# A transformer-and-RWKV layer on one core: one of ten triangular inverses moved from the input projection to the attention stage

## The chip, the cores and the metric

The kernel runs on one core of one Trainium2 chip. The metric is the device time of one execution in microseconds. TensorE (PE) multiplies matrices, VectorE (DVE), ScalarE (ACT) and GpSimd (POOL) work element by element, and SP issues most of the DMAs. Every engine takes its instructions in the order that was fixed when the program was compiled, so an instruction that waits holds up all that stands behind it on its engine, and a DMA that waits on SP holds up all later DMAs of SP.

## The reference

One layer over 2048 latent tokens of width 1024 with a prefix of 256 context tokens. A modulated layer norm feeds one input projection, whose columns go to eight neighbourhood-attention heads (a window of 8 by 16 grid cells plus all context keys) and to eight RWKV-7 heads, which scan the tokens in both directions:

```
S = S * w_t - (S kk_t)(kk_t * a_t)^T + v_t k_t^T ;  y_t = S r_t
```

Both halves are joined, projected, normalised, and followed by a squared-ReLU MLP and a second norm.

## The kernel before, in words

The scan is done in 36 chunks of 64 tokens for each direction d. Within a chunk the delta rule needs the inverse of a triangular 64x64 matrix for each head. These inverses are made ahead of the scan by `solve(d, q0)` (L731 on). The first number is the direction, the second the first of 32 chunk-and-head-pair entries, four to a chunk: `(0, 96)` covers chunks 24 to 31, `(0, 112)` chunks 28 to 35.

A solve is a generator; each call of it emits one piece. In order: DMAs that bring the matrices from the DRAM tensor LB into the tile `mp` (L741) and a clearing of part of the DRAM tensor XB (L749); 31 pairs of DVE instructions, a product into `stmp` (L758) and a row sum into `xp` (L759), which grow from 1 to 961 elements a partition and each read what the one before wrote; an ACT copy `yp` (L763); DMAs out to XS, YS and XB and back in transposed (L767 to L789); a pause of `swait` calls; two rounds of 64 small matmuls, each with an ACT copy behind it (L798, L799); and the DMAs of the last block to XB (L802). All tiles of a solve come from a pool with one buffer each, so two solves overlap little.

The ten solves are spread over the program by the table `SOLVES` (L38). The **input projection** (`phase1`) goes over the tokens in three parts; each is a list of 27 jobs, each of which projects 128 columns of w_in (L448, L466) and works on the result on DVE and ACT: shifts, RWKV terms, rotary embedding (L710 to L715, which ends in a DMA to KR or Q). After each of a job's two pieces `side()` calls the current solve once. Two solves run beside the second part and three beside the third. With `swait` 2 a solve takes 17 calls.

The **attention stage** (first half of `tail`) interleaves three things: 134 steps of `attention()`, of which the first 128 each begin one attention tile (`front`: the product of queries and keys L979, with context keys L982, maximum, exponent, and one scaling on POOL, L997) and finish an earlier one (`back`); 28 steps of the scan in both directions (`chain_pre` loads and prepares a chunk, its inverse `xz` from XB included, L1111 to L1147; `chain_main` advances the state, L1166 to L1195); and `side()`, called after each attention step, which advances the five solves that are left. With `SWAIT` 6 a solve takes 21 calls there. Before step 1 of the attention its own loads must be made and split: keys `kr` (L909 to L911), queries `qz` (L951 to L954), biases `bu` and `bm` (L930 to L934). After the stage the output projection begins (`out_init`), whose tiles take the place in memory of those of the solves and the attention.

The scheduler of the tile framework puts the instructions of all engines into their final order from the order of the program text, from their dependences, and from a timeline of its own.

Of the kernel before, what the change touches and what calls it, by code (L numbers as in the profile page):

```python
# [34 lines left out]
XAT = ("K", 1)  # L35
SPEED = 1

SOLVES = [[(0, 0), (1, 0)], [(1, 112), (1, 96), (0, 96)], [(0, 32), (0, 64), (1, 64), (1, 32), (0, 112)]]  # L38
ASTEPS = 128 + LAG + 4
MID = 28  # L40
SWAIT = 6
# [18 lines left out]
class Kern:  # L60
# [151 lines left out]
    def phase1(self):  # L212
        nc, tc, a = self.nc, self.tc, self.a
        with ExitStack() as es:
# [28 lines left out]
            for n, (sb, b) in enumerate(jobs):  # L243
                if b == jobs[0][1]:
# [3 lines left out]
                    if nxt > 1:  # L248
                        self.sq += [self.solve(*x) for x in SOLVES[nxt - 2]]
                if n == 4:  # L250
# [555 lines left out]
    def tail(self):  # L806
        nc, tc, a = self.nc, self.tc, self.a
        eb, ex = ExitStack(), ExitStack()
        with ExitStack() as ep:
            with ExitStack() as eo:  # L810
                with ExitStack() as ec:

                    self.yacc = [self.pool(ec, "yacc0", 1, side="right").tile([128, 4, 1024], F32, name="yacc0"), None]
                    self.seen = [False] * NCH
                    self.ch1 = self.pool(ec, "ch1", 1, side="right")
                    self.ch2 = self.pool(ec, "ch2", 2, side="right")
                    self.psG = self.pool(ec, "psG", 2, space=PSUM, side="right")
                    self.psR = self.pool(ec, "psR", 1, space=PSUM, side="right")
                    order = [list(range(36)), [3, 2, 1, 0] + list(range(35, 3, -1))]
                    with ExitStack() as ea:  # L820
                        self.sv = self.pool(ea, "sv2", 1)
                        self.at1 = self.pool(ea, "at1", 1)
                        self.at2 = self.pool(ea, "at2", 2)
                        self.psA = self.pool(ea, "psA", 1, space=PSUM)
                        self.psS, self.psname = self.psG, "psg"
                        self.sq = [self.solve(*x) for x in SOLVES[2]]
                        self.speed = 1
                        self.swait = SWAIT
                        self.attn_init()
                        self.chain_init()  # L830
                        at = self.attention()
                        n = 0
                        next(at)
                        self.chain_pre(0, order)
                        next(at)
                        n = 2
                        for s in range(MID):
                            self.chain_pre(s + 1, order)
                            for d in range(2):
                                want = (2 * s + d + 1) * 134 // (2 * MID)  # L840
                                h = (n + want) // 2
                                while n < h:
                                    next(at)
                                    n += 1
                                    self.side()
                                self.chain_main(d, s, order[d])
                                while n < want:
                                    next(at)
                                    n += 1
                                    self.side()  # L850
                        for _ in at:
                            pass
                        assert not self.sq
                    self.psO = self.pool(ep, "psO", 4, space=PSUM)
                    self.chain_pre(MID + 1, order)
                    self.out_init(eo)
                    tiles = self.out_tiles()
                    n = 0
                    for s in range(MID, 36):
                        if MID < s < 35:  # L860
                            self.chain_pre(s + 1, order)
                        for d in range(2):
                            self.chain_main(d, s, order[d])
                            want = 12 * (2 * (s - MID) + d + 1) // (2 * (36 - MID))
                            while n < want:
                                next(tiles)
                                n += 1
                self.psN = self.pool(ep, "psN", 4, space=PSUM, side="right")
                self.base = self.pool(eb, "base", 1, side="right")
                self.xp = self.pool(ex, "xp", 1, side="right")  # L870
                self.uk = self.base.tile([128, 8, 256], F32, tag="uk", name="uk")
                self.xu = {}
                for pr in MORD[:3]:
                    self.xu[pr] = [self.xp.tile([128, 4, 512], F32R, name="x%s%d" % (v, pr)) for v in "hl"]
                self.w1 = {}
                self.w1load(0)
                todo = list(range(8))
                more = True
                while more:
                    for m in todo[:2]:  # L880
                        self.xstep(0, m // 2, m % 2)
                    del todo[:2]
                    more = next(tiles, 0) is None
                assert not todo
        with ExitStack() as e1:
            self.mlp1(e1)
        ex.close()
        with ExitStack() as em:
            self.mlp2(em)
        eb.close()  # L890
# [1036 lines left out]
```

## Time and profile before

| | us |
|---|---|
| median of three runs | 3481.47 |
| the three runs | 3479.99 to 3482.71 |
| the profiled execution, its own time | 3474.77 |
| its span, first to last instruction | 3472.9 |
| PE busy | 3196.9 (92%) |
| DVE busy | 2610.7 (75%) |
| mean granted TensorE clock | 0.96 |

By the trace the input projection ends about 1004 us from the span's start, the attention stage runs to about 1797 us, the output projection follows, and then the two MLP products. The profiled execution is 6.7 us shorter than the median, so every sum below is made against 3474.77 and then carried to the median. "Busy" counts an engine as busy while an instruction is in it. The bound of a stage is read from the waits in that stage, not from the busy shares of the whole span.

### The profile page before, as it was taken

The page shows a single profiled execution, that of the slowest core. Times are in us where ns is not written, and L with a number is a line of the kernel's source. Part 1 is how long each engine was busy: PE and PEld are TensorE (multiplying, and loading weights), DVE is VectorE, ACT ScalarE, POOL GpSimd, SP SyncE. Part 2 cuts the span into 40 slices and gives each one's busy share as a digit, 9 for nine tenths or more (in the row PEclk, how much of TensorE's full clock was granted, in tenths as well). Part 3 has the DMA queues.
Part 4 walks back from the last instruction along what each step waited for, and adds up shares of the span by engine and source line. Part 5 has one row for each costly group of instructions (what it writes and reads, how often), then busy time and mean ns, then how long its engine had stood idle before and what let it go on. Part 6 is the DMA issues. An engine that isn't in the chain of part 4 may idle for free.

```text
span 3472.9 us, 65271 instructions
## 1 busy us (share of the span) xinstructions
PE 3196.9 (92%) x25176; PEld 2602.5 (75%) x25176; DVE 2610.7 (75%) x4907; ACT 1523.3 (44%) x2891; POOL 507.8 (15%) x535
## 2 busy tenths in 40 slices
PE   7999999899957988999979987999999989999998
PEld 3878888789755766776766765777788868888886
DVE  5567977979697668668559867867776757899888
ACT  4555565456433544444442122343433344337433
POOL 0000000000013454544433321000000000010001
PEclk9999999899978999999999988999999999999999
DMA  7487366636776464554354646566644445546442
GB/s 251 133 244 215 90 172 174 195 86 172 188 179 152 110 147 117 134 126 118 97 165 149 182 151 204 196 198 209 217 146 157 141 181 168 162 148 223 143 154 76
DMA packets 765338, 561.67 MB, mean 162 GB/s; under 512 B 380412, under 2 KB 653564, under 8 KB 763620
## 3 DMA queue, kind: packets, MB, share of 16 engines
q1 hardware_dynamic: 691738, 523.14, 51.7%
q10 hardware_dynamic: 73290, 34.37, 3.5%
q8 instruction: 198, 3.24, 0.4%
q14 instruction: 112, 0.92, 0.1%
HBM read 359.70 MB, written 197.66 MB: 160 GB/s over the span
## 4 chain that ended last, share of the span: by engine, by line
PE 66%; DVE 15%; DMA 10%; issue 3%; ACT 3%; SPq 3%; ACTq 0%; POOL 0%; DVEq 0%; POOLq 0%
PE psm L448 13%; PE psa L1524 10%; PE psqb L1722 7%; PE psqa L1722 7%; PE psb L1524 5%; PE ops L1339 3%; PE pse L1524 2%; DMA ks<-AR 2%; PE psv L1044 2%; PE psm L466 2%; PE psg L1134 1%; DVE stmp L758 1%; PE pst L1015 1%; PE psl L979 1%; DMA qz<-Q 1%
## 5 line engine op out<-in xcount | busy, mean ns | idle before, releaser
L448 PE MATMUL psm<-xh,wh 128*128 128x386 f32 (+1 forms) x1104 | 381.0, 347 | 15.5 <-ACT row L451 10.3
L448 PE MATMUL psm<-xl,wh 128*128 128x386 f32 (+1 forms) x1104 | 381.1, 345 | 2.2 <-DVE xl L419 2.1
L448 PE MATMUL psm<-xh,wl 128*128 128x386 f32 (+1 forms) x1104 | 376.9, 341 | 0.0
L448 PEld LDWEIGHTS psm<-xh,wh 128*128 128x128 f32 x1104 | 210.2, 191 | 41.5 <-ACT row L451 18.8
L448 PEld LDWEIGHTS psm<-xl,wh 128*128 128x128 f32 x1104 | 210.6, 191 | 17.6 <-DVE xl L419 7.6
L448 PEld LDWEIGHTS psm<-xh,wl 128*128 128x128 f32 x1104 | 210.5, 191 | 5.0 <-issue 3.7
L1524 PE MATMUL psa<-xh,w1h 128*128 128x512 f32 x512 | 204.6, 400 | 9.2 <-ACT w1h L1455 4.8
L1524 PE MATMUL psa<-xl,w1h 128*128 128x512 f32 x512 | 203.2, 397 | 0.0
L1788 POOL TENSOR_TENSOR acc<-acc,g 128x1024 f32<-128x1024 f32 x8 | 28.9, 3639 | 1188.4 <-DVE acc L1731 1188.4
L1524 PE MATMUL psa<-xh,w1l 128*128 128x512 f32 x512 | 202.2, 396 | 0.0
L1672 ACT CAST ah<-al 128x1024 fp32r<-128x1024 f32 x98 | 102.9, 1050 | 222.8 <-DMA al<-HU 197.0
L1673 DVE TENSOR_TENSOR al<-al,ah 128x1024 fp32r<-128x1024 f32 x98 | 121.4, 1239 | 88.4 <-ACT ah L1672 88.3
L758 DVE TENSOR_TENSOR stmp<-mp,xp 128x9 f32<-128x9 f32 (+30 forms) x310 | 168.0, 542 | 23.8 <-DMA mp<-LB 11.0
L434 DVE TENSOR_TENSOR wl<-wst,wh 128x1024 fp32r<-128x1024 f32 x81 | 98.8, 1219 | 89.1 <-ACT wh L433 76.0
L1455 ACT CAST w1h<-w1s 128x512 fp32r<-128x512 f32 x96 | 59.6, 621 | 239.4 <-DVE w1s L1444 82.2
L1722 PE MATMUL psqa<-uh,ah 128*128 128x512 f32 x400 | 155.0, 391 | 4.2 <-ACT uh L1628 3.2
L1722 PE MATMUL psqb<-uh,ah 128*128 128x512 f32 x384 | 149.8, 393 | 9.8 <-ACT uh L1628 9.8
L1134 PE MATMUL psg<-ks,bkc 64*64 64x128 f32 (+1 forms) x1152 | 99.2, 292 | 63.3 <-DMA ks<-AR 61.0
L1722 PE MATMUL psqa<-ul,ah 128*128 128x512 f32 x400 | 157.3, 393 | 0.0
L1722 PE MATMUL psqa<-uh,al 128*128 128x512 f32 x400 | 156.8, 392 | 0.0
L759 DVE TENSOR_REDUCE xp<-stmp 128x3 f32<-128x9 f32 (+30 forms) x310 | 154.0, 497 | 3.4
L1722 PE MATMUL psqb<-ul,ah 128*128 128x512 f32 x384 | 151.0, 393 | 0.0
(393 smaller groups left out, 8890.5 us busy)
## 6 DMA issues: line engine op xcount, KB each, us to landing
al<-HU SPq DMA_DIRECT2D x106, 512.0 KB
wst<-in_w_in SPq DMA_DIRECT2D x81, 512.0 KB
w<-in_mlp_w SPq DMA_DIRECT2D x32, 1024.0 KB
wp<-in_mlp_w SPq DMA_DIRECT2D x32, 1024.0 KB
wmod<-in_w_mod SPq DMA_DIRECT2D x48, 512.0 KB
HU<-p SPq DMA_DIRECT2D x96, 256.0 KB
HU<-s SPq DMA_DIRECT2D x84, 256.0 KB
bkc<-BK SPq DMA_DIRECT2D x36, 512.0 KB
```

What stands on the lines that cost most here:

```text
L434: nc.vector.tensor_tensor(wl, w, f32(wh), ALU.subtract)
L448: nc.tensor.matmul(ps[:, :y - x], lhsT=s[:, k, :], rhs=m[:, k, x:y], start=(i == 0), stop=(i == 23))
L466: nc.tensor.matmul(ps[:, :y - x], lhsT=s[:, k, :], rhs=m[:, k, lo + x:lo + y], start=(i == 0), stop=(i == 23))
L758: nc.vector.tensor_tensor(tv, mp[:, i:i + 1, lo:lo + n].to_broadcast([128, n, n]), xp[:, lo:lo + n, lo:lo + n], ALU.mult)
L759: nc.vector.tensor_reduce(xp[:, lo:lo + n, i], tv, AX.X, ALU.add)
L1044: nc.tensor.matmul(cell["ps"][hs, i0:i0 + n, :], lhsT=vt[:, hs], rhs=x, start=first, stop=last, skip_group_check=True)
L1134: nc.tensor.matmul(ps[u, p, 0:w], lhsT=bk[o, d, p, u], rhs=ks[h][o, d, p, 0:w], start=True, stop=True)
L1339: nc.tensor.matmul(ps, lhsT=x[:, k, :], rhs=w[:, k, c], start=(i == 0), stop=(i == 23))
L1524: nc.tensor.matmul(ps, lhsT=w[:, k, :], rhs=x[:, k, :], start=(i == 0 and pr in (1, 5, 2)), stop=(i == 11), skip_group_check=True)
L1672: fs += [lambda: nc.scalar.copy(ah, f32(al)), fb[0], lambda: V.tensor_tensor(al, f32(al), f32(ah), ALU.subtract), fb[1]]
L1673: lambda: V.tensor_tensor(al, f32(al), f32(ah), ALU.subtract), fb[1]]
L1722: nc.tensor.matmul(ps, lhsT=x[:, c, s], rhs=y[:, c, :], start=(i == 0 and new), stop=(i == 5 and end), skip_group_check=True)
```

## The change

Solve `(0, 96)` leaves the third part's list and goes to the attention's, before `(0, 112)`. The attention's list, now six, is not called before its sixth step.

```
-SOLVES = [[(0, 0), (1, 0)], [(1, 112), (1, 96), (0, 96)], [(0, 32), (0, 64), (1, 64), (1, 32), (0, 112)]]
+SOLVES = [[(0, 0), (1, 0)], [(1, 112), (1, 96)], [(0, 32), (0, 64), (1, 64), (1, 32), (0, 96), (0, 112)]]
+
+SFIRST = 6
...
                         at = self.attention()
+                        sq, self.sq = self.sq, []
                         n = 0
...
                                 while n < h:
                                     next(at)
                                     n += 1
+                                    if n == SFIRST:
+                                        self.sq = sq
                                     self.side()
                                 self.chain_main(d, s, order[d])
                                 while n < want:
                                     next(at)
                                     n += 1
+                                    if n == SFIRST:
+                                        self.sq = sq
                                     self.side()
```

In the attention stage the solves' calls began at step 3 and ended at step 107 (five times 21 calls). They now begin at step 6, and the last call of the six is at step 131 of 134. Line numbers of the changed kernel are 2 higher up to the attention stage and 7 higher behind it; the rows below print each kernel's own.

The rows below show how the compiled order moves. First the SP queue at the start of the attention stage, from the loads of the first scan chunk on (`ks`, `bkc`, `SV`, `xz` belong to the scan, `vw` to the attention; `XS`, `YS`, `svx`, `svs` and `XB<-yp` to the moved solve). Before:

```order
L1121 DMA SV<-VT 64x4x64 x4
L1123 DMA xz_11143<-XB 128x2x256
L918 DMA vw<-VN 32x8x128 x7
L767 DMA XS_82<-xp 128x1024
L918 DMA vw<-VN 32x8x128 x3
L768 DMA YS_84<-yp 128x1024
L773 DMA XB<-yp 32x32x32 x4
L785 DMA svx<-LB 32x16x32 x4
L788 DMA svs<-XS_82 32x16x32
L789 DMA svs<-YS_84 32x16x32
```

After the change, from the same place:

```order
L1128 DMA SV<-VT 64x4x64 x4
L1130 DMA xz_10881<-XB 128x2x256
L925 DMA vw<-VN 32x8x128 x16
L1118 DMA bkc<-BK 128x2x512
L1125 DMA ks_11025<-AR 64x4x64 x2
L1125 DMA ks_11026<-AR 64x4x64 x2
L1128 DMA SV<-VT 64x4x64 x4
L1130 DMA xz_10882<-XB 128x2x256
L1118 DMA bkc<-BK 128x2x512
L1125 DMA ks_11192<-AR 64x4x64 x2
```

The moved solve's DMAs no longer stand between the loads of the first and the second scan chunk.

Then PE from the last product of the input projection to the first attention tile (`psc` the last RWKV terms, `psg` the preparation of scan chunks, `psb` the moved solve, `psl` and `psx` an attention tile). Before, the end of the projection:

```order
L448 MATMUL psm<-xh,wl 128x386
L684 MATMUL psc<-ar,bk 64x64 x16
L691 MATMUL psc<-kds,bones 128x256
L1134 MATMUL psg<-ks_11201,bkc 64x64
L1147 MATMUL psg<-ident,bkc 128x128 x4
```

and, after the rest of the first chunk's preparation, up to the second chunk's (whose 14 further rows of `psg` stand ahead of the first `psl`):

```order
L1147 MATMUL psg<-ident,bkc 128x128 x4
L798 MATMUL psb<-svs,svx 32x32 x64
L1134 MATMUL psg<-ks_11287,bkc 64x64
L1147 MATMUL psg<-ident,bkc 128x128 x4
L798 MATMUL psb<-svs,svx 32x32 x64
L1134 MATMUL psg<-ks_11288,bkc 64x64
```

After the change:

```order
L450 MATMUL psm<-xl,wh 128x386
L450 MATMUL psm<-xh,wl 128x386
L986 MATMUL psl<-kr_10876,qz_10870 128x256
L989 MATMUL psx<-kc_10898,qz_10870 128x256
L986 MATMUL psl<-kr_10876,qz_10871 128x256
L986 MATMUL psl<-kr_10877,qz_10870 128x256
L1141 MATMUL psg<-ks_10939,bkc 64x64
L1154 MATMUL psg<-ident,bkc 128x128 x4
```

The attention's first tile now follows the last product of the projection directly, and no matmul of a solve stands between them.

Last, SP at the end of the attention stage, after the change (`XB<-t` is the last DMA of the last solve, `hsel` the first load of the output projection):

```order
L1118 DMA bkc<-BK 128x2x512
L804 DMA XB<-t_21303 32x16x32 x4
L1122 DMA ks_21660<-AR 64x2x512
L1122 DMA ks_21661<-AR 64x2x512
L1130 DMA xz_10882<-XB 128x2x256
L1128 DMA SV<-VT 64x4x64 x4
L1273 DMA hsel_21742<-in_hsel 128x32
```

Before, the last `XB<-t` stood 34 rows ahead of `hsel`; it now stands 5 rows ahead, among the loads of the last scan chunk of this stage.

## Rows read from the trace of the kernel before

**Rows 1.** Busy time of each engine in stretches from the projection's end on.
```profile
core 0: us, PE busy (x) PEld busy (x) DVE busy (x) ACT busy (x) POOL busy (x), PEclk, DMA share, GB/s
950.00:1001.00 51.00, 50.74 (x359) 48.16 (x361) 49.52 (x111) 20.67 (x39) 0.52 (x1) 1.00 0.58 168
1001.00:1034.00 33.00, 1.19 (x20) 0.65 (x15) 30.91 (x60) 6.53 (x11) 5.71 (x7) 0.55 0.88 210
1034.00:1068.00 34.00, 12.38 (x332) 10.37 (x332) 27.40 (x57) 4.78 (x6) 7.49 (x9) 0.50 0.86 189
...
1674.00:1778.00 104.00, 99.66 (x1361) 76.98 (x1359) 58.22 (x196) 48.59 (x138) 41.67 (x52) 0.98 0.32 83
```
**Rows 2.** PE in order of time, 1002 to 1070 us: start, length, what, idle before.
```profile
1003.39 0.70 PE L691 MATMUL psc<-kds,bones 128*128 128x256 f32 x2 [1.89 <-DVE kds L661]
1034.54 0.44 PE L1134 MATMUL psg<-ks,bkc 64*64 64x64 f32 x2 [30.45 <-DMA ks<-AR]
...
1052.65 0.31 PE L798 MATMUL psb<-svs,svx 32*32 32x32 f32 x2 [12.92 <-DMA svs<-XS]
...
1062.87 0.45 PE L1134 MATMUL psg<-ks,bkc 64*64 64x64 f32 x2 [5.76 <-DMA ks<-AR]
...
1068.05 1.01 PE L979 MATMUL psl<-kr,qz 128*128 128x256 f32 x3
```
**Rows 3.** SP's issues in order of time, 1024 to 1059 us: start, length, what.
```profile
1024.86 0.32 SPq L715 DMA_DIRECT2D KR<-rot  x1
...
1027.66 3.45 SPq L1118 DMA_DIRECT2D ks<-AR  x4
...
1039.66 0.34 SPq L767 DMA_DIRECT2D XS<-xp  x1
...
1058.81 2.57 SPq L1118 DMA_DIRECT2D ks<-AR  x4
```
**Rows 4.** DVE in order of time: split of the first keys, and the last bias.
```profile
1015.46 1.49 DVE L911 TENSOR_TENSOR kr<-kr,kr 128x1280 fp32r<-128x1280 f32 x1 [0.23 <-ACT kr L910]
...
1031.28 2.05 DVE L934 TENSOR_TENSOR bm<-bu,rmask 128x384 f32<-128x384 f32 x2
```
**Rows 5.** DVE busy (x): 1001 to 1041 us all, L758, L759; then L758 to 1088.
```profile
1001.00:1041.00 40.00, 37.76 (x72) 0.54 0.87 204
1001.00:1041.00 40.00, 9.37 (x13) 0.54 0.87 204
1001.00:1041.00 40.00, 8.86 (x14) 0.54 0.87 204
...
1041.00:1088.00 47.00, 15.36 (x26) 0.70 0.67 152
```
**Rows 6.** L758 (DVE busy) of one solve beside the projection, in attention; L759 likewise.
```profile
792.00:882.00 90.00, 15.54 (x31) 1.00 0.63 170
1186.00:1255.00 69.00, 18.41 (x31) 1.00 0.48 115
...
792.00:882.00 90.00, 15.40 (x31) 1.00 0.63 170
1186.00:1255.00 69.00, 15.38 (x31) 1.00 0.48 115
```
**Rows 7.** L997 on POOL, one an attention tile: (x) is tiles begun in the stretch.
```profile
1170.00:1674.00 504.00, 73.75 (x88) 0.96 0.53 126
1674.00:1778.00 104.00, 15.53 (x20) 0.98 0.32 83
1186.00:1255.00 69.00, 10.52 (x13) 1.00 0.48 115
...
1557.00:1630.00 73.00, 8.24 (x11) 0.98 0.40 101
1255.00:1305.00 50.00, 7.77 (x10) 1.00 0.73 162
...
1630.00:1674.00 44.00, 7.28 (x11) 0.96 0.60 144
```

More of the change, by code (lines that the diff above doesn't have):

```diff
@@ L36 @@
 SPEED = 1
-SOLVES = [[(0, 0), (1, 0)], [(1, 112), (1, 96), (0, 96)], [(0, 32), (0, 64), (1, 64), (1, 32), (0, 112)]]
+SOLVES = [[(0, 0), (1, 0)], [(1, 112), (1, 96)], [(0, 32), (0, 64), (1, 64), (1, 32), (0, 96), (0, 112)]]
+SFIRST = 6
 ASTEPS = 128 + LAG + 4
@@ L831, in tail @@
                         at = self.attention()
+                        sq, self.sq = self.sq, []
                         n = 0
@@ L844, in tail @@
                                     n += 1
+                                    if n == SFIRST:
+                                        self.sq = sq
                                     self.side()
@@ L849, in tail @@
                                     n += 1
+                                    if n == SFIRST:
+                                        self.sq = sq
                                     self.side()
```

## The prediction

> **What bounds the kernel now.** I read the busy time by stretches first, then PE in order of time where it stands still, then SP's issues there, then DVE. The input projection is bound by PE: in its last 51 us PE is busy for 50.7, with DVE full beside it [rows 1]. The attention stage is close to PE's bound where no solve runs: 99.7 of 104 us in its last stretch, with DVE at 58 [rows 1]. Between the two lies a hole. From 1001 to 1034 us PE works 1.2 us, from 1034 to 1068 us 12.4, while DVE is busy for 30.9 and 27.4 [rows 1]. The reader should see what holds PE, step by step: it ends the projection at 1004.1, waits 30.45 us for `ks`, the first scan chunk's load, prepares that chunk, waits 12.9 us for `svs`, the transposed blocks of solve (0, 96), waits 5.8 us for the second chunk's `ks`, and begins the first attention tile (L979) at 1068.05 [rows 2]. All three waits lead to SP or DVE. The first `ks` is issued at 1027.66, a few places behind the last rotary outputs (KR, 1024.86), which DVE makes late. The second is issued at 1058.81, behind the DMAs of (0, 96), which begin with `XS` at 1039.66, once DVE has ended its 31 pairs [rows 3]. DVE is late because it does (0, 96) in between: of 37.8 busy us from 1001 to 1041, 9.4 and 8.9 are pairs of solves [rows 5].
>
> **The change part by part.** *Removed beside the projection.* (0, 96) goes with all its instructions: its 62 DVE instructions, ACT's three copies, 128 matmuls, and 28 DMAs on SP. The projection itself gains nothing: PE is full there [rows 1], and I cost this at zero.
>
> *The restart of PE.* The compiled order has the first attention tile right behind the last product of the projection; the last `psc` matmuls move ahead of eleven of its products. PE should end the projection near 1002 us (1004.1 less the 1.9 us for which it waited for DVE [rows 2]). What then stands before the first tile is DVE's own work: 37.76 - 9.37 - 8.86 = 19.5 us of rotary, key, query and bias work in 1001 to 1041 us [rows 5], which from 1002 ends at 1021.5. Some of it will already be done, since DVE loses (0, 96) before 1001 too. I take 1020, a gain of 48 us on 1068. Bounds: no earlier than about 1016, since the second split of the keys ends at 1017 today and waits not for a solve but for the copy before it [rows 4], a gain of 52; and no later than 1034.5, when PE is let go today [rows 2], a gain of 33.5. The biases, ready at 1033 today [rows 4], are in the 19.5.
>
> *What the hole held.* PE's 12.4 us in 1034 to 1068 [rows 1] were the preparation of two scan chunks and the matmuls of (0, 96). About 9 of them, the preparation, now lie among the first attention tiles. The first tiles wait for DVE and ACT in any case, so I take 5, between 0 and 9.
>
> *Two more solves beside the attention, not one.* Today five are called in the attention stage, but the first of them, (0, 32), did 26 of its 31 L758 from 1041 to 1088 us [rows 5], so mostly while PE stood still. Starting at step 6, (0, 32) runs beside tiles, as does (0, 96). What does a solve cost there? From 1170 to 1674 us, with the DVE work of four solves, 88 tiles take 504 us, 5.73 each; the last 20 without one take 104 us, 5.20 each [rows 7]. That is 0.53 x 88 / 4 = 11.6 us a solve, the lower bound. The upper: in the four stretches that hold the pairs (the first and last stand in [rows 7]) 45 tiles take 283 us, 6.29 each; in the four between them 44 take 205 us, 4.66 each; 1.63 us x 11.25 tiles = 18.3. The stretches between also catch up what the others held back, so the truth is nearer the lower end. I take 14, two of them 28 (23 to 37).
>
> This is the place for a rule that speaks against the change. One solve's L758 take 15.5 us beside the projection and 18.4 in the attention, where POOL is at work, while L759 stay at 15.4 [rows 6]. The Trainium skill (SBUF — State Buffer, "SBUF: two separate sides") says that a DVE operation with two SBUF inputs and a GpSimd operation that reads SBUF shut each other out of a shared port pair for a whole instruction; L758 has two inputs, L759 one, and the trace agrees. By the rows beside the projection two solves would be 61.9 us of DVE, by those in the attention 67.6. My 28 is read from tiles of the attention, so it holds this already.
>
> *Steps and deadlines.* The pieces of (0, 96) end at step 110, and the scan's chunk 24 is loaded right behind them; that `xz` is used only a scan step later (4.8 attention steps, some 25 us at 5.2), so it costs nothing unless SP is then still behind. The last DMA of (0, 112) comes at step 131 instead of 107 and now stands five rows ahead of the output projection's loads. SP may stand there for a matmul round and a copy. I take 1 us, between 0 and one attention tile, 6.
>
> *Sum.* -48 + 5 + 28 + 1 = **-14 us**. Against the profiled execution that is 3474.8 - 14 = 3460.8. That execution lies 6.7 us under the median, so for the median: 3481.5 - 14 = **3467.5 us**. All favourable ends give -52 + 0 + 23 + 0 = -29, all adverse ones -33.5 + 9 + 37 + 6 = +18.
>
> **The rivals.**
> - *DVE sets the attention stage (slower).* If each solve there costs its whole DVE time, 18.4 + 15.4 = 33.8 us [rows 6], two cost 67.6, and -48 + 5 + 67.6 + 1 = +26, so 3507. The point from which it decides: above 21 us a solve (42 / 2) the change loses. For it: the rule of the port pair above makes DVE's work longer in just this stage, and POOL works 41.7 of 104 us there [rows 1]. Against: the four solves in 1170 to 1674 us cost 18.3 each at the most [rows 7]. Chance 0.08.
> - *The loads set the restart (no change).* If DMAs, not DVE, decide when the first tile can begin, PE starts at 1034.5 as now: -33.5 + 5 + 28 + 1 = 0, so 3482. For it: keys and queries can be loaded only when the projection's tiles are free, and the DMA engines are 0.88 busy in 1001 to 1034 [rows 1]. Against: two solves' own DMAs leave that stretch, and `ks` was issued late, not landing late [rows 3]. Chance 0.17.
> - *The attention hides more (faster still).* DVE idles 104 - 58.2 = 45.8 us over 20 tiles, 2.3 a tile [rows 1, 7]. If a solve over 11 tiles uses all of that, 33.8 - 25.2 = 8.6 is left, and -48 + 5 + 17 + 1 = -25, so 3456. Against: the stretches with a solve never ran so well. Chance 0.15.
>
> **How the numbers follow.** The forecast has the remaining 0.60. About 0.2% (7 us) is what a measurement of this kernel can tell from no change. Of the forecast's 0.60 some 0.55 lies under -7 us; with the third rival's 0.15 and 0.02 of the second, faster is 0.72. Same has 0.05 of the forecast and 0.13 of the second rival, 0.18; slower the first rival and 0.02 of the second, 0.10. The range runs from -31 (just past the favourable ends) to +5 (past the second rival), 3450 to 3486.5; it leaves out the first rival and the tails.
>
> **What would show it.** In the profile of the changed kernel the first L986 (the attention's L979) should start near 1020 us, the wait of 30 us for `ks` and that for `svs` at the hole should be gone, and no pair of a solve should stand on DVE between the last rotary output and the first tile. The tiles should advance at about 6.3 us where a solve's pairs run, in six such stretches instead of four, and at about 5 elsewhere; the attention stage should end some 14 us earlier than 1797. The forecast is wrong if PE's first tile is later than 1034, if the six stretches take over 7 us a tile, or if the output projection's first loads wait for the last `XB<-t`.

## The result and the profile after

The changed kernel takes **3429.53 us** (median of 4 runs, 3427.45 to 3432.04), the kernel before beside it 3480.73 (4 runs, 3474.66 to 3482.71): a ratio of 0.9857, 95% interval 0.9845 to 0.9868. It is faster, by 51 us in the medians. The forecast was 3467.5 with a range of 3450 to 3486.5: the direction was right, the size was not. The profiled execution took 3430.26 us with a span of 3428.5, 44.4 less than the span before.

Busy time by stretches, with the columns of [rows 1]:
```profile
core 0: us, PE busy (x) PEld busy (x) DVE busy (x) ACT busy (x) POOL busy (x), PEclk, DMA share, GB/s
950.00:1001.00 51.00, 49.27 (x354) 46.00 (x353) 47.30 (x105) 21.71 (x42) 0.00 (x0) 1.00 0.64 184
1001.00:1034.00 33.00, 14.88 (x108) 11.76 (x108) 21.75 (x48) 9.50 (x20) 7.45 (x9) 0.59 0.88 217
1034.00:1068.00 34.00, 27.47 (x350) 22.05 (x350) 20.65 (x70) 17.52 (x50) 18.04 (x23) 0.90 0.73 152
1674.00:1778.00 104.00, 91.43 (x1482) 71.77 (x1477) 68.54 (x164) 45.42 (x111) 35.10 (x41) 0.91 0.55 154
```
From 1001 to 1068 us PE now works 42.4 us where it worked 13.6 [rows 1]. (The last stretch is no longer free of solves: the sixth runs in it.) PE in order of time there, the answer to [rows 2]; lines of the attention stage stand 7 higher than before, so L986 is the L979 of before and L1141 its L1134:
```profile
1002.39 0.34 PE L450 MATMUL psm<-xh,wl 128*128 128x386 f32 x1
1017.19 0.58 PE L986 MATMUL psl<-kr,qz 128*128 128x256 f32 x1 [14.46 <-ACT qz L960]
...
1021.95 0.79 PE L986 MATMUL psl<-kr,qz 128*128 128x256 f32 x2 [3.66 <-DVE qz L961]
1022.67 0.47 PE L1141 MATMUL psg<-ks,bkc 64*64 64x64 f32 x2
...
1041.21 0.45 PE L1141 MATMUL psg<-ks,bkc 64*64 64x64 f32 x2 [4.51 <-DMA ks<-AR]
```
The waits of 30.45 us for `ks` and of 12.92 for `svs` are gone. The first attention tile starts at 1017.19 in place of 1068.05 and waits 14.46 us for ACT's copy of the first queries. The same chain on SP and ACT, beside [rows 3]:
```profile
1008.22 0.60 SPq L717 DMA_DIRECT2D KR<-rot  x1
1009.43 5.85 SPq L958 DMA_DIRECT2D qz<-Q  x6
...
1017.89 2.55 SPq L1125 DMA_DIRECT2D ks<-AR  x4
...
1034.20 2.57 SPq L1125 DMA_DIRECT2D ks<-AR  x4
```
```profile
1016.51 1.14 ACT L960 CAST qz<-qz 128x512 fp32r<-128x512 f32 x2 [1.77 <-DMA qz<-Q]
```
The last `KR` is issued at 1008.22, 16.6 us earlier than before, and nothing of a solve stands between the two loads of `ks`.

**The account by stages**, from the first or last product of each stage in PE's order of time (`psm` is the last product of the projection, `psl` the first of the attention, `ops` the first of the output projection, `psa` the first of the block behind it). The first `ops` before, then after:
```profile
1799.94 1.03 PE L1225 MATMUL ops<-ysq,hsel 128*8 128x256 f32 x4
```
```profile
1765.23 1.46 PE L1232 MATMUL ops<-ysq,hsel 128*8 128x256 f32 x4
```

| us | psm to psl | psl to ops | ops to psa | psa to the end |
|---|---|---|---|---|
| before | 68.0 | 731.9 | 352.6 | 1320.3 |
| after | 14.8 | 748.0 | 344.8 | 1318.4 |

The last `psm` starts at 1000.1 before and 1002.4 after. So the difference of the spans is +2.3 - 53.2 + 16.2 - 7.8 - 1.9 = -44.4. The gap gave what was expected of it. The attention stage, with one whole solve more and (0, 32) no longer in the gap, grew by 16.2 us, where the forecast had 33, and ends 34.7 us earlier, where the forecast had 14. The output projection, which the forecast left as it was, is 7.8 us shorter; what shortens it, no run here tells.

**The tiles.** L1004 on POOL, one an attention tile, as in [rows 7]: first two of the six stretches in which pairs run, then two of those between them.
```profile
1064.00:1141.00 77.00, 11.49 (x12) 0.98 0.49 133
...
1641.00:1710.00 69.00, 9.31 (x11) 0.91 0.31 83
```
```profile
1141.00:1182.00 41.00, 6.29 (x8) 0.88 0.75 160
...
1593.00:1641.00 48.00, 7.61 (x10) 1.00 0.64 140
```
All six together: 67 tiles in 419 us, 6.25 each; the seven stretches outside them: 63 tiles in 290 us, 4.60 each. As forecast, some 6.3 us a tile in six stretches and some 5 elsewhere. But L1004 is the last instruction of a tile's first half and runs on POOL. The same stretches for the tile's first products on PE (L986, three a tile), again two beside the pairs, then two between:
```profile
1064.00:1141.00 77.00, 11.19 (x42) 0.98 0.49 133
...
1641.00:1710.00 69.00, 9.32 (x36) 0.91 0.31 83
```
```profile
1141.00:1182.00 41.00, 5.41 (x21) 0.88 0.75 160
...
1593.00:1641.00 48.00, 6.04 (x24) 1.00 0.64 140
```
This is the reading that decides the case. All six stretches have 229 of these products, that is 76.3 tiles of 5.49 us; the seven outside have 151, 50.3 tiles of 5.76. Where tiles begin, on PE, they take no more time beside the pairs than elsewhere. (Outside, 21.0 of the 290 us go to the solves' own products, L800, of which none runs beside the pairs; without them it is 5.35 us a tile, still within 0.14.) What is late there is POOL: its scaling starts up to 19.8 us after the tile's first product beside the second solve's pairs, and 4.4 us after it behind them. Nor does PE wait more; all engines, first beside the pairs, then outside:
```profile
sum 419.00, PE 385.13 PEld 299.17 DVE 388.51 ACT 198.79 POOL 213.66; mean PE 64.19 PEld 49.86 DVE 64.75 ACT 33.13 POOL 35.61
```
```profile
sum 290.00, PE 258.72 PEld 207.12 DVE 149.33 ACT 148.94 POOL 128.66; mean PE 36.96 PEld 29.59 DVE 21.33 ACT 21.28 POOL 18.38
```
DVE is busy for 388.5 of 419 us beside the pairs, but PE stands still for 33.9 us there, 8%, and for 31.3 of 290 us outside, 11%.

### The profile page after: what moved, and what is told of

It is laid out like the page before. It is cut to its first block, busy times and chain, and to the rows that moved or that the text cites. A ratio compares the mean times of both kernels' runs of the same rounds, so it can differ in the third digit from the quotient of the medians.

```text
span 3428.5 us, 65249 instructions
## 1 busy us (share of the span) xinstructions
PE 3193.7 (93%) x25176; PEld 2605.3 (76%) x25176; DVE 2603.2 (76%) x4907; ACT 1523.1 (44%) x2891; POOL 511.6 (15%) x535
## 5 line engine op out<-in xcount | busy, mean ns | idle before, releaser
L760 DVE TENSOR_TENSOR stmp<-mp,xp 128x1 f32<-128x1 f32 (+30 forms) x310 | 179.2, 578 | 18.3 <-POOL xp L752 6.8
L761 DVE TENSOR_REDUCE xp<-stmp 128x1 f32<-128x1 f32 (+30 forms) x310 | 153.9, 496 | 3.3
L1729 PE MATMUL psqb<-uh,al 128*128 128x512 f32 x384 | 150.3, 391 | 0.0
```

The lines of the kernel that those rows point to most:

```text
L760: nc.vector.tensor_tensor(tv, mp[:, i:i + 1, lo:lo + n].to_broadcast([128, n, n]), xp[:, lo:lo + n, lo:lo + n], ALU.mult)
L761: nc.vector.tensor_reduce(xp[:, lo:lo + n, i], tv, AX.X, ALU.add)
L1729: nc.tensor.matmul(ps, lhsT=x[:, c, s], rhs=y[:, c, :], start=(i == 0 and new), stop=(i == 5 and end), skip_group_check=True)
```

## The experiments

Twelve kernels. "Gap" is `psm` to `psl` in the profiled execution, "stage" `psl` to `psa`, so the attention stage and the output projection, and "attention" the part of it up to `ops`.

| kernel | start, pause | time us | ratio to before (95%) | gap | stage | attention |
|---|---|---|---|---|---|---|
| before | - | 3478 to 3481 | 1 | 68.0 | 1084.5 | 731.9 |
| after | 6, 6 | 3429.5 | 0.9857 (0.9845 to 0.9868) | 14.8 | 1092.9 | 748.0 |
| e1 move alone | 3, 6 | 3461.4 | 0.9943 (0.9929 to 0.9958) | 15.8 | 1131.3 | 773.7 |
| e2 late start alone | 6, 6 | 3455.2 | 0.9931 (0.9917 to 0.9945) | 68.5 | 1066.4 | 716.3 |
| e3 no pairs | 6, 6 | 3418.1 | 0.9819 (0.9805 to 0.9833) | 15.2 | 1083.8 | 724.0 |
| e4 without (0, 96) | 6, 6 | 3424.1 | 0.9840 (0.9825 to 0.9856) | 14.7 | 1088.7 | 743.2 |
| e5 | 4, 6 | 3454.9 | 0.9921 (0.9897 to 0.9945) | 16.0 | 1125.3 | 766.2 |
| e6 | 5, 6 | 3428.3 | 0.9846 (0.9826 to 0.9866) | 15.8 | 1096.9 | 752.7 |
| e7 no pairs | 3, 6 | 3410.9 | 0.9804 (0.9779 to 0.9829) | 15.0 | 1079.4 | 721.9 |
| e8 before, no pairs in (0, 96) | - | 3420.1 | 0.9826 (0.9806 to 0.9847) | 12.0 | 1071.9 | 729.1 |
| f1 | 6, 5 | 3430.4 | 0.9863 (0.9837 to 0.9889) | 15.7 | 1090.7 | 744.8 |
| f2 | 6, 4 | 3442.7 | 0.9907 (0.9876 to 0.9938) | 14.8 | 1108.2 | 765.8 |
| f3 no pairs in (0, 32) | 3, 6 | 3429.6 | 0.9859 (0.9831 to 0.9886) | 15.1 | 1099.5 | 755.8 |
| f4 | 10, 5 | 3448.6 | 0.9915 (0.9889 to 0.9942) | 14.9 | 1113.1 | 763.9 |

### The two parts of the change, one at a time

The move alone (e1), against the changed kernel:
```diff
-SFIRST = 6
+SFIRST = 3
```


> The solve (0, 96) is moved as in the change, but the attention's list begins at step 3 as before, not at step 6. Theory A (the hole at the start of the attention stage comes from (0, 96) alone; the 23 us that the changed kernel gains between tiles 20 and 100 come from where the solves' pairs fall against the attention's steps): the first attention tile at 1017 to 1025 us as in the changed kernel, the middle as slow as before, so some 3445 to 3460 us. Rival B (the middle gained because the schedule behind a clean start is better, whatever the step): within 7 us of the changed kernel, 3423 to 3437. Rival C (the late start is what frees the beginning): the first tile later than 1035 and over 3455 us.

The late start alone (e2), against the changed kernel:
```diff
-SOLVES = [..., [(1, 112), (1, 96)], [(0, 32), (0, 64), (1, 64), (1, 32), (0, 96), (0, 112)]]
+SOLVES = [..., [(1, 112), (1, 96), (0, 96)], [(0, 32), (0, 64), (1, 64), (1, 32), (0, 112)]]
```


> All three solves stay beside the projection's third part, and only the start of the attention's list is put off to step 6. Theory A: the hole stays (the first tile at 1055 to 1068 us), the middle gains its 23 us, but (0, 32) now runs beside tiles for some 14 us: 3465 to 3475 us. Rival B: nothing is gained in the middle, 3480 to 3495. Rival C: the hole closes without the move, under 3450.

Measured: 3461.4 and 3455.2, so -17 and -23 us; the two add up to -40, and together they give -51. By the ratios it is -20, -24 and -50, a difference of 6 that is not clear of the intervals. PE in order of time in e1, then in e2:
```profile
1011.93 0.58 PE L986 MATMUL psl<-kr,qz 128*128 128x256 f32 x1 [15.45 <-ACT qz L960]
```
```profile
1033.03 0.45 PE L1141 MATMUL psg<-ks,bkc 64*64 64x64 f32 x2 [30.83 <-DMA ks<-AR]
...
1050.48 0.31 PE L800 MATMUL psb<-svs,svx 32*32 32x32 f32 x2 [12.31 <-DMA svs<-XS]
...
1061.54 0.44 PE L1141 MATMUL psg<-ks,bkc 64*64 64x64 f32 x2 [6.24 <-DMA ks<-AR]
...
1066.71 0.96 PE L986 MATMUL psl<-kr,qz 128*128 128x256 f32 x3
```
The move alone closes the gap, the late start does nothing to it. What the late start gives, it gives behind the gap: e2's stage is 18 us shorter than before's, and after's 38 shorter than e1's. It does not take (0, 32) out of the gap. The first products of the pairs (L760) in e2, in the stretches of [rows 5]:
```profile
1001.00:1041.00 40.00, 10.38 (x16) 0.52 0.92 217
1041.00:1088.00 47.00, 14.37 (x24) 0.68 0.63 142
```
Those of (0, 32) run from 1021 to 1080 us, as before (1023 to 1081); only the four solves behind it start later, by one to four tiles. The expectation had (0, 32) beside tiles for some 14 us, and e2 came out 10 us under its range. In e1 (0, 32) runs beside tiles, from 1047 us, with the start at 3: it is the move that brings it there. In e1 the stage is 47 us longer, and nearly all of the closed gap is lost again.

### What the solves cost beside the tiles

e3 leaves 30 of the 31 pairs out of all six attention solves, so that the inverses' columns are not computed, and keeps the transfers and products:
```diff
...
-            nc.vector.tensor_tensor(tv, mp[:, i:i + 1, lo:lo + n]...
-            nc.vector.tensor_reduce(xp[:, lo:lo + n, i], tv, AX.X, ALU.add)
+            if self.swait != SWAIT or n == 1:
+                nc.vector.tensor_tensor(tv, mp[:, i:i + 1, lo:lo + n]...
+                nc.vector.tensor_reduce(xp[:, lo:lo + n, i], tv, AX.X, ALU.add)
```


> The attention's six solves make the first of their 31 pairs and leave out the other 30, so their inverses are not computed; DMAs, copies and matmuls stay. Price theory P1 (a solve's DVE work costs the attention stage 14 to 18 us, as I took and as the first and the last solve of the changed kernel seem to show): 84 to 108 us less than the changed kernel, 3322 to 3346. Rival P2 (DVE's idle time takes the pairs up, a solve costs some 4 us, which is what the two more cost in all): 20 to 30 us less, 3400 to 3410.

e4 leaves the solve (0, 96) out altogether; its part of XB is cleared instead:
```diff
-..., [(0, 32), (0, 64), (1, 64), (1, 32), (0, 96), (0, 112)]]
+..., [(0, 32), (0, 64), (1, 64), (1, 32), (0, 112)]]
...
+        if (d, q0) == (0, 0):
+            for j in range(2):
+                nc.sync.dma_start(self.XB[:, 0, 96 + 16 * j:112 + 16 * j, :].rearrange("s q t -> s (q t)"), xf)
```


> The solve (0, 96) is left out altogether (the inverses of forward chunks 24 to 27 are zeros, written once by two DMAs at the first solve); the other five run as in the changed kernel from step 6 on. P1: one solve is worth 11 to 18 us, 3411 to 3419. P2: 4 us, 3424 to 3428.

Measured: 3418.1 and 3424.1. Six solves' pairs cost 11 us end to end, about 2 each, less than either price that was stated for them; one whole solve costs 5, as the smaller price had it, and the intervals of e4 and after overlap. The stretch from the first to the last tile, 127 tiles on, all engines, in after and then in e3:
```profile
1026.90:1735.80 708.90, 643.75 (x9519) 506.19 (x9520) 537.74 (x1558) 347.74 (x943) 342.14 (x384) 0.96 0.55 131
```
```profile
1020.70:1706.10 685.40, 640.35 (x9503) 500.61 (x9505) 366.89 (x1197) 347.85 (x943) 321.06 (x384) 0.96 0.57 134
```
171 us of DVE's work are gone, and the tiles end 23.5 us sooner, 3.9 a solve; the attention stage is 24.0 us shorter, and the output projection takes 15.1 of them back (359.9 against 344.8). Without any pair the tiles take 5.40 us on average against 5.58. And POOL's two paces are gone: the tiles that ran beside pairs in after (66 of them, counted from scaling to scaling) take 5.42 here, the others 5.37. Counted on PE, from first product to first product, there were no long tiles beside the pairs to begin with: 5.47 beside them and 5.84 elsewhere in after, 5.43 and 5.45 in e3.

### Where a solve's pieces fall

> The changed kernel with its attention solves let in from the fourth tile on, in place of the sixth. Theory A (where in the run of tiles and chain steps a solve's pieces fall decides what the same six solves cost PE; the cost changes step by step of the start): the time lies anywhere between the start at 3 (3461) and the start at 6 (3430), 3435 to 3455, and the waits of PE between tile 0 and tile 127 go with it (82 us at 3, 65 us at 6, by the difference of the stretch and PE's busy time). Theory C (it is only that pieces before the sixth tile lie in the start of the attention stage): 4 is nearly as dear as 3, 3452 to 3462, and the loss against the changed kernel is there already by tile 24 or so. If the start did not matter and the run at 3 was an accident: 3430 within 5.

> The changed kernel with its attention solves let in from the fifth tile on. Theory A (alignment): anywhere between 3425 and 3455, not in order with the starts at 3, 4 and 6 necessarily; tile leads that part from those of the changed kernel in the middle of the stage, not at its start. Theory C (only the start of the stage counts): between the start at 4 and the start at 6, in order, 3435 to 3450. No effect of the start: 3430 within 5.

The edit is the one constant, `SFIRST = 4` and `SFIRST = 5`. Measured: 3454.9 and 3428.3. One tile makes 27 us. 3 and 4 are alike, and so are 5 and 6. (A and C are from here on the theories of these two expectations.) 3454.9 fits both; the early loss that C asks for is not there: counted by the starts of tiles on PE, e5 is 1 us ahead of after at tile 24, then 8 behind at tile 40, 15 at 70 and 20 at the last. 3428.3 fits A and not C.

> The start at tile 3 with six solves whose 30 of 31 VectorE pairs are left out (so the inverses' columns are not computed; loads, stores and products stay). It tells what makes the start at 3 dearer than the start at 6 by 31 us. If it is VectorE's pairs that fall on PE's waits there, the 31 us go: 3418 within 6, the same as the start at 6 without pairs. If it is the solves' transfers and products and the places where SP's queue gets them, most of the 31 us stay: 3440 to 3450.

e7 is e3 with `SFIRST = 3`: 3410.9. Without the pairs the start at 3 costs nothing more than that at 6, so the 32 us between them are the pairs' doing, not the transfers'. Against e1 the pairs of six solves cost 50.5 us here, 8.4 each, where they cost 2 each with the start at 6. The longest of PE's waits from the first tile to the last, in e1 and then in after:
```profile
PE psg L1141 <- DMA ks<-AR: 27.1, 23, 6.7
PE psg L1154 <- DVE ks L1148: 11.2, 5, 8.3
PE psl L986 <- DVE mx L996: 5.7, 4, 2.3
PE pst L1029 <- ACT pt L1023: 5.7, 8, 1.8
PE psg L1154 <- DVE stmp L760: 5.4, 1, 5.4
```
```profile
PE psg L1141 <- DMA ks<-AR: 22.3, 17, 4.5
PE pst L1029 <- ACT pt L1023: 7.3, 10, 2.2
PE us L1194 <- DVE SV L1190: 5.4, 4, 4.2
PE psx L989 <- ACT S L999: 5.3, 7, 1.8
PE psg L1154 <- DVE ks L1148: 4.4, 8, 1.5
```
No single wait holds the difference. In e1 PE is busy for 657.0 of 738.7 us at a granted clock of 0.94, in after for 643.7 of 708.8 at 0.96: 17 us more of idling, 13 more of busy time for the same work at the lower mean clock. Counted by PE's matmuls from the first tile on, e1 is 2 us behind after 1000 of them, 9 after 2500, 21 after 5000 and 31 after 7000; the loss does not lie at the stage's beginning.

> The changed kernel with a pause of 5 calls in place of 6 within each attention solve (SWAIT = 5): the first solve's pieces stay where they were, the second to sixth come in one to five tiles earlier. Theory A (each start of a solve falls well or badly among the tiles and scan steps, wherever in the stage): the time scatters, 3420 to 3460, with a shift of 5 us or more either way. Theory C (what costs is only that the first solve begins too early in the stage): 3429 within 5, as with the pause of 6.

> The changed kernel with a pause of 4 calls: the second to sixth solves come in two to ten tiles earlier, and the last ends ten tiles before the attention does. Theory A: scatters, 3420 to 3460. Theory C: 3429 within 5. If the transposed loads of a solve land later than four tiles after their issue, PE waits for svs (3 us in all in the changed kernel) and the time rises by 10 to 30 us.

> The changed kernel with its solves let in from the tenth tile on, with a pause of 5 calls so that all end in time. Theory C (the later the first solve, the better the beginning of the stage): 3415 to 3430. Theory A: scatters, 3420 to 3460, without order in the start. As a candidate for a kernel faster than the changed one it has to stay under 3424.

The edits are `SWAIT = 5`, `SWAIT = 4`, and `SFIRST = 10` with `SWAIT = 5`. Measured: 3430.4, 3442.7 and 3448.6. A later start is not better, and earlier second to sixth solves are worse once and the same once. In f2 PE waits 5.0 us for `svs` (1.2 in after), too little for the 13 us. f1 came out as C had it, f2 and f4 lie outside C's ranges and inside A's. Over the seven kernels with all the work and the move the times are 3428 to 3461, mean 3442.

> The start at tile 3 (3461) with 30 of 31 VectorE pairs of the first attention solve, (0, 32), left out (its inverse is not computed; transfers and products stay). It tells whether the 31 us by which the start at 3 is dearer than the start at 6 lie with the first solve. Theory C (the beginning of the stage, where PE, VectorE and the loads are already short): 25 us or more go, 3425 to 3436. Theory A (all six solves fall badly): only this solve's share goes, some 8 us of 50, 3447 to 3457.

f3 is e1 with the condition `(d, q0) != (0, 32) or n == 1` ahead of the pairs: 3429.6, 32 us less than e1. That is theory C's number, for the pairs of a single solve, where a solve's pairs cost 2 us on average with the start at 6. With f2, f4, e6 and the counts along the stage against C, what stands is that leaving out one solve's pairs can be worth 30 us, spread over the whole stage. Each of these edits also changes the compiled order: in the traces of e5 and e6, one tile apart, 8366 of PE's 25,176 places have a product of another line or tile. Whether the place of the pairs costs this by itself, or the order that the scheduler makes around it, was not told apart.

### What made the gap

> The kernel before, with 30 of 31 VectorE pairs of the solve (0, 96) beside the projection left out (that block's inverse is not computed); its loads, stores, waits and products stay where they were. It tests what made the hole ahead of the first tile (the first product of the stage at 1068 us, after waits of 30 us for ks and 13 us for svs). If the pairs held VectorE, and so the store that the later loads on SP's queue stand behind: the first product comes at 1018 to 1035, the 30-us wait is gone, and the total falls by 15 to 45 us (3435 to 3463). If it is the solve's transfers and calls by their place in the queue, pairs or no pairs: the first product stays at 1050 to 1068 and the total at 3470 to 3480.

e8 is the kernel before, with the condition `(d, q0) != (0, 96) or n == 1` ahead of the pairs. Measured: 3420.1, a fall of 60 us, where 15 to 45 were expected of the pairs. PE's first tile and SP's first `ks` in e8:
```profile
1023.20 0.58 PE L980 MATMUL psl<-kr,qz 128*128 128x256 f32 x1 [11.64 <-ACT qz L954]
```
```profile
1023.46 2.55 SPq L1119 DMA_DIRECT2D ks<-AR  x4
1040.02 2.57 SPq L1119 DMA_DIRECT2D ks<-AR  x4
```
The gap is 12.0 us. All transfers, calls and products of (0, 96) are still there, but they too run earlier: `XS` goes out at 927.4 us in place of 1039.7, the products run from 969.6 to 994.0 in place of 1052.7 to 1066.2, and the pairs of (0, 32) begin at 1059 in place of 1023, beside tiles. So the gap hangs on the pairs of (0, 96). Whether the time on DVE makes it, or the stores, transposed loads and products that come late behind the pairs, e8 does not tell apart, and its compiled order is another one too. The gap gives 56 us of the fall and a stage shorter by 13 another part, while the projection's last product comes 11 us later. e8 also gives a size to what is left to gain: the changed kernel is 9 us above this one, which does not compute (0, 96)'s inverse, 5 above one without the solve, and 11 above one without any pair in the attention stage. No version here beats the changed kernel beyond its interval with all of the work done.

## Why the prediction was wrong in size

- **The restart of PE: right, in part by luck.** -48 was forecast, with bounds of -52 and -33.5; the first tile starts 50.9 us earlier, and the time of 1020 that was given for it came out as 1017. The reason holds for the first part alone: DVE's last rotary output goes out at 1008.22, and the loads of the queries stand behind it on SP (from 1009.43). From there PE waits for these loads and ACT's copy of them, which have no term in the sum, while the rest of the 19.5 us of DVE's own work, the biases, ends at 1020.9, after the first tile has begun. So the rival on the loads had part of the path right, with a restart at 1034.5 where it was 1017.2.
- **The projection gains nothing: nearly right.** Its last product starts 2.3 us later in the profiled execution of after. In the ten experiments without (0, 96) beside the projection it starts at 991 to 997 us against 1000.1 before, so some 4 us may be gained there.
- **What the hole held, +5, and two more solves beside the attention, +28: here is the failed step.** 33 us were forecast for the attention stage, 16.2 were measured, and from `psl` to `psa` 8.4. The step was the price "What does a solve cost there?", 11.6 to 18.3 us, read from tiles: "1.63 us x 11.25 tiles = 18.3" and "0.53 x 88 / 4 = 11.6 us a solve, the lower bound". Both take POOL's scalings (L997) for the pace of PE. POOL falls behind beside the pairs and catches up between them, so its count makes tiles long and short while PE goes on as before. By the same method the changed kernel gives (6.25 - 4.60) x 67 / 6 = 18.4 us a solve; leaving the pairs out gives 3.9 within the tiles and 2 end to end. What was called the lower bound was none: of the 20 tiles of its last stretch in [rows 7] one had begun at 1673.91, before the stretch; the 19 begun in it take 5.47 us each, near the 5.40 of e3 with no pairs at all, and (5.73 - 5.47) x 88 / 4 is 5.7 us. A view that was at hand before would have told it. It is L979 in the kernel before, the first products of a tile, three a tile. The first two rows and the last two are each a stretch with solve pairs and the one behind it:
```profile
1186.00:1255.00 69.00, 10.50 (x42) 1.00 0.48 115
1255.00:1305.00 50.00, 5.47 (x23) 1.00 0.73 162
1557.00:1630.00 73.00, 9.93 (x39) 0.98 0.40 101
1630.00:1674.00 44.00, 6.43 (x24) 0.96 0.60 144
```
  That is 4.9, 6.5, 5.6 and 5.5 us a tile, with no long tiles beside the pairs. Over the prediction's eight stretches (283 and 205 us) L979 has 150 and 107 products: 5.66 us a tile beside the pairs and 5.75 between them, where 6.29 and 4.66 were read. Between them 14.4 of the 205 us are the solves' own products (L798); without these it is 5.34, so the pairs make a tile 0.32 us longer, and the 12.5 tiles of a solve 4.0 us, not 12 to 18. Leaving the pairs out of e3 gave the same, 24.0 / 6 in the attention stage. Nor is there one price: a solve's pairs cost 2 us on average with the start at 6, 8.4 with the start at 3, and 32 for (0, 32) alone there.
- **What the forecast did not have: the start itself.** SFIRST = 6 was read as only a later date for (0, 32), which brings it beside tiles; by e1 and e2 the move does that. The scatter over starts and pauses (33 us between the best and the worst of seven) is larger than the whole forecast. With the start at 3 the same move gives -17 us, close to the -14 forecast, and by other terms: gap -52, stage +47. That nearness is chance. Why the same pairs cost so much more or less by where they start stays open.
- **Steps and deadlines, +1: right.** The time behind the output projection is 1.9 us shorter, and no wait of the output projection for the last transfers of (0, 112) shows.
- **The rivals.** DVE as the bound of the stage fell: DVE is full beside the pairs (388.5 of 419 us), but taking 171 us from it shortens the tiles by 23.5. "The attention hides more" was the right case; its price, 8.6 us a solve, is twice what the attention stage shows with the start at 6 (24.0 us for the pairs of six solves, 4.0 each).
- **The port pair.** The Trainium skill's rule (SBUF — State Buffer, "SBUF: two separate sides") was held to be inside the 28. The traces agree with it in direction: a POOL scaling of a tile takes 106.44 / 127 = 838 ns in after and 98.20 / 127 = 773 ns in e3, where DVE's pairs are gone. What these 65 ns do to the time was not tested.

## What to carry to other kernels

Count the units of a pipeline on the engine whose time is to be priced. A count on an engine further down shows that engine falling behind and catching up: here 6.25 and 4.60 us a tile on POOL, 5.49 and 5.76 on PE. Put PE's idle time in both kinds of stretches beside it before a long tile is charged to what runs beside it. A gap in PE can be worth nearly its length when what holds it moves to a stage with room, here DVE, busy for 482 of 702 us from the first to the last tile before; but the same move gave back 47 of the 52 us of the closed gap with the start at 3, and 8 of 53 with the start at 6. So when an edit shifts work in a compiled order, try its neighbours too: one tile earlier or later was worth 27 us, twice what was forecast for the whole change.

## What the runs showed of the hardware that was not expected

Nothing new of the chip decides here, but two numbers stand. The 31 L760 products of one solve take 21.5, 19.9 and 16.8 us (the last without the first product, which ended before the stretch) in three stretches of the changed kernel's attention stage, against 15.5 beside the projection in [rows 6]: the same instructions take up to two fifths longer there, and differ by a quarter among solves of one stage. And the granted clock of PE is 0.59 from 1001 to 1034 us and 0.90 from 1034 to 1068: after the 14.8 us of standing still, at the end of a stretch at 1.00, the first tiles ran at a mix of PE's two levels, 1.2 and 2.4 GHz.
